# Fixed places for the q/k turns in a hybrid SSM and attention layer, the values' products behind the granule, and V in two tiles

## The chip, the cores and the metric

The kernel runs on one core of a Trainium2 chip. Its time is the device time of one execution in microseconds (us), taken as the median of several runs. A profile is one further execution with the hardware profiler on. PE is the matrix engine (TensorE), with PEld for its weight loads; DVE is VectorE, ACT is ScalarE, POOL is GpSimd, and SP issues most of the transfers.

## The reference

One decoder layer on 512 positions of width 1024, in float32. A state-space branch and an attention branch share one input projection, are gated, summed and projected again.

```python
h = rms_norm(x, norm_w)
u_s, z_s, q, k, v, z_a, r_s, r_a = split(h @ w_in)
y_s = s5_branch(u_s, ...)                         # complex diagonal scan, GELU, GLU
y_s = (y_s * silu(z_s)) @ w_ssm_out
q, k = rope(rms_norm(q, q_norm_w)), rope(rms_norm(k, k_norm_w))   # per head of 64
y_a = dilated_attention(q, k, v)                  # 3 groups x 8 heads
y_a = (y_a * silu(z_a)) @ w_attn_out
x = x + (sigmoid(r_s) * y_s + sigmoid(r_a) * y_a) @ w_o
```

In `dilated_attention`, group 0 looks at the last 128 positions, group 1 at every 4th of the last 512 and group 2 at every 16th of the last 2048 (129 keys each, as far as they exist). The three outputs of a head are combined, weighted by their softmax denominators.

## The kernel before

Precision: each float32 operand of the large products is split into a rounded high part and a low remainder (`split`, lines 106 to 112: ACT writes `w_hi`, DVE `w_lo`), and `mm3` (line 122) makes three products, high by high, high by low and low by high. Line 63 is the helper through which every product is recorded, line 67 the one for every transpose on PE.

Weights come in the order of a list, `plan`. `get_w` (line 180) hands out the next piece and starts the load and the split of pieces up to two further on. The split pieces have three buffers.

The attention part is the loop `for hp in range(NP)` at line 1094, over four pairs of heads. What pair `hp` needs in one turn of the loop:

- `scores(hp)` (line 921): products of q and k (`sps`), then for each block of 128 positions a masked minimum on DVE (line 929) and an exponential on ACT (line 931) into the tile `Pt`. POOL moves the sums between partitions (lines 961 and 978), a short chain on DVE joins the denominators of the groups, and DVE scales `Pt` (line 985). `kind` 0 is group 0, `kind` 1 is the two dilated groups.
- `qk_first` (line 884): q and k of the groups 0 and 1 for the next pair, by `wide_granule` (line 817). A granule has four accumulators `pss[r]` (`pj`, one PSUM bank each, all four of the pool `ps_p`) and runs over four pieces of weights `kq`. One (`kq`, `r`) is called a block here: six products of 512 columns. ACT copies the results into `raws[0]` and `raws[1]` (line 891) and squares them (line 879), DVE sums the squares (line 882), and `qk_norm` (line 834) makes the reciprocal root on DVE (lines 115 to 120, 841), scales (line 846) and rotates on POOL (lines 852 to 857). Only after line 857 is a raw tile ready.
- `qk_second(hp + 1, mid)` (line 896): a second granule with q and k of group 2 and v of the groups 1 and 2. Between its pieces it calls `mid(kq)`, which traces `qk_turn(0, ...)`, `qk_turn(1, ...)` and `values`. Behind the granule, for each `r`, it copies the raw tile (line 903), squares, and copies v into the tile `V` (line 905), then norms.
- `qk_turn` (line 859): turns one raw tile for q (`a` = 0) and k (`a` = 1), four transposes on PE into one PSUM bank each (`qtp`), then a high part by ACT (line 873) and a low part by DVE (line 874).
- `values(hp, Pt, V)` (line 988): eight groups of `Pt` transposes (`ptp`), 30 transposes in all, copied to SBUF by ACT (`ptb`, line 1027) and DVE (line 1029) in turn, and 60 products with V into one accumulator `ot`; then `at` (line 1036) takes the gate.
- `v0_unit` (line 585): v of group 0 for the next pair, a projection into one `pj` bank, turned later by its `finish`; then `qk_turn(2, ...)`.

`qtp`, `ptp`, `vtp` and `sps` share the pool `ps_g`, which has three banks at this stage. `at`, the squares (`qsq`) and the evicted v (`vt`) share the tag `t2k` with six buffers. `V` is one tile with one buffer: the next pair's v can be written only when the last product with the old one is done.

What sets the order: the text is traced in program order, but a planner then fixes each engine's order by going through the program with lengths of its own and giving an engine what is ready and stands first. So a place in the text is a preference, not the place on the engine. `queued()` (line 69) adds an order by hand: what its block traces on PE is issued behind the last PE instruction traced before it. Before the change only the turn of group 1 is queued so.

## Time and profile before

| | |
|---|---|
| median of 3 runs | 737.64 us (736.49 to 738.57) |
| span of the profiled execution | 732.6 us |
| its own time beside the span | not given on the page; the median lies 5.1 us above the span |
| PE busy | 699.6 us, 95% |
| mean granted TensorE clock | 0.993 |
| loop over the pairs | about 434 to 667 us of the span |

The span counts from the first to the last instruction of the profiled execution. The engines' busy times overlap, so they don't add up to it. A row of a timeline has the start, the length, the engine, the line in the code, the operation, the output and inputs by their names in the code, the count, and in brackets the idle time before it with what ended it. A row of waits has the total in us, the count and the longest. In a row of stretches the first number is the length; the engines' busy times with their counts, the granted clock (1.00 is full speed), the share of the DMA engines and GB/s follow.

### The profile page before, as it was taken

To read this page: it belongs to the slowest core of one execution; us is meant where nothing else is said; L and a number is where in the kernel's file an instruction comes from. 1 tells how busy PE (TensorE), PEld (TensorE's weight loads), DVE (VectorE), ACT (ScalarE), POOL (GpSimd) and SP (SyncE) were. 2 spreads that over 40 slices of the span, in tenths; PEclk is the share of its full clock that TensorE was granted. 3 is DMA by queue.
4 is the path that set the end of the run, shared out by engine and by line. 5 is a ranking of instruction groups with operands and counts; after the bars stand their busy time and mean duration, and the time that the engine had idled before them with its cause. 6 is when DMAs were issued, how large, how long until landed. Compare 5 with 4: busy or idle time off the path is not lost.

```text
span 732.6 us, 12680 instructions
## 1 busy us (share of the span) xinstructions
PE 699.6 (95%) x4821; PEld 574.2 (78%) x4821; DVE 457.1 (62%) x912; ACT 314.6 (43%) x631; POOL 191.7 (26%) x346
## 2 busy tenths in 40 slices
PE   2799899999999999999999999999989999999997
PEld 2687688778878787888888888788868877878886
DVE  6759673989946546764335659655664666464832
ACT  6434463332326465442144456537153734443420
POOL 3426540230205343550000316021601250230000
PEclk9999999999999999999999999999999999999999
DMA  8433653564547554455333432222412231326441
GB/s 203 106 96 94 171 144 77 137 149 132 120 131 153 122 103 133 139 168 172 99 100 87 130 87 79 66 58 58 115 31 79 65 89 30 115 73 236 139 144 57
DMA packets 137213, 82.14 MB, mean 112 GB/s; under 512 B 32696, under 2 KB 125632, under 8 KB 137024
## 3 DMA queue, kind: packets, MB, share of 16 engines
q1 hardware_dynamic: 135088, 78.96, 37.5%
q0 software_dynamic: 2048, 2.36, 2.6%
q8 instruction: 38, 0.62, 0.4%
q14 instruction: 23, 0.19, 0.1%
q10 hardware_dynamic: 16, 0.00, 0.0%
HBM read 68.46 MB, written 10.49 MB: 108 GB/s over the span
## 4 chain that ended last, share of the span: by engine, by line
PE 87%; DMA 4%; ACT 3%; DVE 3%; SPq 2%; issue 1%; ACTq 0%
PE pj L63 71%; DMA w_raw<-in_w_in_dram 3%; PE sps L63 3%; PE yps L63 3%; PE ot L63 2%; PE ptp L67 2%; PE kps L63 2%; PE xps L63 1%; PE qtp L67 1%; DMA Uj<-ud 1%; ACT w_hi L108 1%; SPq L442 1%; PE wps L67 1%; ACT qkp L873 1%; DVE w_lo L110 1%
## 5 line engine op out<-in xcount | busy, mean ns | idle before, releaser
L108 ACT ACTIVATE w_hi<-w_raw 128x1024 fp32r<-128x1024 f32 x100 | 106.0, 1061 | 236.8 <-PE pj L63 206.6
L110 DVE TENSOR_TENSOR w_lo<-w_raw,w_hi 128x1024 fp32r<-128x1024 f32 x98 | 124.3, 1268 | 107.9 <-ACT w_hi L108 107.2
L63 PE MATMUL pj<-hT_lo,w_hi 128*128 128x512 f32 (+1 forms) x344 | 132.9, 387 | 3.0 <-DVE hT_lo L251 3.0
L63 PE MATMUL pj<-hT_hi,w_hi 128*128 128x512 f32 (+1 forms) x344 | 132.8, 389 | 2.4 <-ACT V L905 1.4
L63 PE MATMUL pj<-hT_hi,w_lo 128*128 128x512 f32 (+1 forms) x344 | 132.4, 386 | 1.6 <-DVE w_lo L110 1.6
L63 PE MATMUL pj<-w_hi,hT_hi 128*128 128x512 f32 (+1 forms) x288 | 106.5, 372 | 0.0
L63 PE MATMUL pj<-w_lo,hT_hi 128*128 128x512 f32 (+1 forms) x288 | 106.5, 370 | 0.0
L63 PE MATMUL pj<-w_hi,hT_lo 128*128 128x512 f32 (+1 forms) x288 | 106.0, 371 | 0.0
L63 PEld LDWEIGHTS pj<-hT_lo,w_hi 128*128 128x128 f32 x344 | 66.0, 192 | 16.2 <-DVE hT_lo L251 3.9
L63 PEld LDWEIGHTS pj<-hT_hi,w_hi 128*128 128x128 f32 x344 | 65.5, 192 | 16.5 <-ACT V L905 2.1
L63 PEld LDWEIGHTS pj<-hT_hi,w_lo 128*128 128x128 f32 x344 | 65.9, 192 | 15.4 <-DVE w_lo L110 2.3
L63 PEld LDWEIGHTS pj<-w_hi,hT_hi 128*128 128x128 f32 x288 | 54.1, 188 | 10.0 <-issue 0.2
L63 PEld LDWEIGHTS pj<-w_hi,hT_lo 128*128 128x128 f32 x288 | 54.0, 188 | 10.0
L63 PEld LDWEIGHTS pj<-w_lo,hT_hi 128*128 128x128 f32 x288 | 54.0, 188 | 9.8
L931 ACT ACTIVATE Pt<-Pt,st 128x256 f32<-128x256 f32 (+1 forms) x64 | 31.0, 492 | 18.7 <-DVE st L929 18.7
L735 POOL TENSOR_TENSOR kt<-kt,dg 16x128 f32<-16x128 f32 x8 | 4.6, 571 | 125.0 <-ACT kt L734 118.4
L852 POOL TENSOR_TENSOR rt<-qraw,tC 128x256 f32<-128x256 f32 x12 | 14.3, 1189 | 87.7 <-DVE qraw L846 87.4
L739 POOL DMA_DIRECT2D dd<-kt x64 | 33.7, 535 | 2.4 <-POOL kt L735 2.4
L874 DVE SCALAR_TENSOR_TENSOR qkp<-qtp,wcol,qkp 128x512 fp32r<-128x512 f32 (+1 forms) x32 | 23.0, 745 | 13.5 <-ACT qkp L873 13.4
L961 POOL COPY sw<-st 32x4 f32<-32x4 f32 x64 | 12.0, 187 | 73.2 <-ACT Pt L931 70.5
L873 ACT ACTIVATE qkp<-qtp,wcol 128x512 fp32r<-128x512 f32 (+1 forms) x32 | 20.8, 685 | 15.7 <-PE qtp L67 10.4
L277 POOL TENSOR_TENSOR ab<-dd,AT 128x512 f32<-128x512 f32 x16 | 23.0, 1446 | 11.6 <-DVE ab L278 11.6
(263 smaller groups left out, 1289.4 us busy)
## 6 DMA issues: line engine op xcount, KB each, us to landing
w_raw<-in_w_in_dram SPq DMA_DIRECT2D x40, 512.0 KB
w_raw<-in_w_in_dram SPq DMA_DIRECT2D x112, 128.0 KB
w_raw<-in_w_glu_dram SPq DMA_DIRECT2D x8, 512.0 KB
w_raw<-in_w_ssm_out_dram SPq DMA_DIRECT2D x8, 512.0 KB
w_raw<-in_w_o_dram SPq DMA_DIRECT2D x8, 512.0 KB
x_all<-in_x_dram SPq DMA_DIRECT2D x4, 512.0 KB
ud<-uT SPq DMA_DIRECT2D x8, 256.0 KB
Uj<-ud SPq DMA_DIRECT2D x8, 256.0 KB
```

The source lines that it names most:

```text
L63: last[0] = nc.tensor.matmul(*a, **k)
L67: last[0] = nc.tensor.transpose(*a, **k)
L108: act.activation(hi, src, AF.Copy, scale=scale)
L110: e.tensor_tensor(lo, src, hi.bitcast(F32), op=ALU.subtract)
L277: eng.tensor_tensor(tv, a2.unsqueeze(2).broadcast_to(sh), ai, op=ALU.mult)
L442: sp.dma_start(D1[64 * h:64 * h + 64, a], bv[a][h])
L739: pool.dma_start(M[Q * t:Q * t + Q, :, 0:P - Q * t], kt[:, :, t:].rearrange("q g k p -> q g (k p)"))
L852: pool.tensor_tensor(t1, rh[:, :, :, 0:16], cv.broadcast_to([P, NB * 2, 2, 16]), op=ALU.mult)
L873: act.activation(hi, ps[sl], AF.Copy, scale=w)
L874: dve.scalar_tensor_tensor(lo, ps[sl], w, hi.bitcast(F32), op0=ALU.mult, op1=ALU.subtract)
L931: act.activation(o, o, AF.Exp, bias=nm, scale=-1.0, accum_out=st[:, kind, 1, h, b:b + 1])
L961: pool.tensor_copy(sw[32 * r:32 * r + 32, :, :, b], st[32 * b:32 * b + 32, 1, :, :, r])
```

## The change

Three things change, all in the attention loop.

1. `wide_granule` calls `mid(kq, r)` ahead of every block instead of ahead of every piece. `qk_turn` can now trace one half (q or k). The four halves of the turns of group 0 and 1 stand ahead of the blocks (2,3), (3,0), (3,1) and (3,2), each queued behind the block before it on PE, and each of these blocks is queued behind its turn.
2. `values` is traced after `qk_second` as a whole and queued behind the granule. Within it the dilated groups (`kind` 1) come first, so the accumulator starts with them and ends with group 0.
3. `V` becomes two tiles with a tag each: `V[0]` for group 0 and `V[1]` for the dilated groups.

```diff
-            act.copy(V[:, 0].rearrange("p b c -> p (b c)"), pt)
+            act.copy(V[0].rearrange("p b c -> p (b c)"), pt)
...
     def new_v():
-        return big.tile([P, NG, NB, P], F32, name="V", tag="s6a")
+        return (big.tile([P, NB, P], F32, name="V0", tag="s6c"), big.tile([P, 2, NB, P], F32, name="V", tag="s6a"))
...
         for kq in range(4):
-            if mid:
-                mid(kq)
             hi, lo = get_w()
             for r in range(NB):
-                for k in range(2):
-                    kk = 2 * kq + k
-                    mm3(pss[r], th[:, kk, r * P:(r + 1) * P], tl[:, kk, r * P:(r + 1) * P], hi[:, k], lo[:, k],
-                        kk == 0, kk == KT - 1)
+                tied = mid(kq, r) if mid else False
+                with queued() if tied else nullcontext():
+                    for k in range(2):
+                        kk = 2 * kq + k
+                        mm3(pss[r], th[:, kk, r * P:(r + 1) * P], tl[:, kk, r * P:(r + 1) * P], hi[:, k], lo[:, k],
+                            kk == 0, kk == KT - 1)
...
-    def qk_turn(g, raw, QT, KA, KB):
-        for a in range(2):
+    def qk_turn(g, raw, QT, KA, KB, parts=(0, 1)):
+        for a in parts:
...
-            act.copy(V[:, 1:3, r], pss[r][:, 256:512].rearrange("p (g c) -> p g c", g=2))
+            act.copy(V[1][:, :, r], pss[r][:, 256:512].rearrange("p (g c) -> p g c", g=2))
...
-                        first = kind == 0 and b == 0
+                        first = kind == 1 and b == 0 and k == 0
                         pe.matmul(o, v, pts[h][:, (2 * i + k) * P:(2 * i + k + 1) * P], start=first,
-                                  stop=kind == 1 and b == NB - 1 and k == 1, skip_group_check=True)
+                                  stop=kind == 0 and b == NB - 1 and k == 1, skip_group_check=True)
         n = 0
-        for kind in range(2):
+        for kind in (1, 0):
...
-            def mid(kq):
-                if kq == 1:
-                    qk_turn(0, raws[0], *QK)
-                if kq == 2:
-                    with queued():
-                        qk_turn(1, raws[1], *QK)
-                if kq == 3:
-                    values(hp, Pt, V)
+            steps = {(2, 3): (0, 0), (3, 0): (0, 1), (3, 1): (1, 0), (3, 2): (1, 1)}
+
+            def mid(kq, r):
+                if (kq, r) not in steps:
+                    return False
+                g, a = steps[kq, r]
+                with queued():
+                    qk_turn(g, raws[g], *QK, parts=(a,))
+                return True
             raw, V_next = qk_second(hp + 1, mid)
+            with queued():
+                values(hp, Pt, V)
             V = V_next
             finv = v0_unit(hp + 1, V)
             qk_turn(2, raw, *QK)
```

More of the change, by code (lines that the diff above doesn't have):

```diff
@@ L1 @@
 import math
-from contextlib import ExitStack
+from contextlib import ExitStack, nullcontext
 import numpy as np
@@ L598, in v_granule @@
         for b in range(2):
-            act.copy(V[:, 1:3, 2 * b:2 * b + 2], pss[b].rearrange("p (r g c) -> p g r c", r=2, g=2))
+            act.copy(V[1][:, :, 2 * b:2 * b + 2], pss[b].rearrange("p (r g c) -> p g r c", r=2, g=2))
     def new_v():
-        return big.tile([P, NG, NB, P], F32, name="V", tag="s6a")
+        return (big.tile([P, NB, P], F32, name="V0", tag="s6c"), big.tile([P, 2, NB, P], F32, name="V", tag="s6a"))
     scn = big.tile([P, 4096], F32, name="scn", tag="s3")
@@ L866, in qk_turn @@
             if a == 0 or g == 0:
-                parts = [(slice(0, P), QT[0][:, g], QT[1][:, g]) if a == 0 else (slice(0, P), KA[0], KA[1])]
+                ends = [(slice(0, P), QT[0][:, g], QT[1][:, g]) if a == 0 else (slice(0, P), KA[0], KA[1])]
             else:
-                parts = [(slice(64 * h, 64 * h + 64), KB[0][64 * h:64 * h + 64, g - 1, h],
+                ends = [(slice(64 * h, 64 * h + 64), KB[0][64 * h:64 * h + 64, g - 1, h],
                           KB[1][64 * h:64 * h + 64, g - 1, h]) for h in range(2)]
-            for sl, hi, lo in parts:
+            for sl, hi, lo in ends:
                 w = wcol[sl, g, a:a + 1]
@@ L1001, in pv @@
                         if kind == 0:
-                            v = V[:, 0, b - 1 + k, po]
+                            v = V[0][:, b - 1 + k, po]
                             o = ov[po, b]
                         else:
-                            v = V[:, 1 + k, b, po]
+                            v = V[1][:, k, b, po]
                             o = ot[po, b * P:(b + 1) * P]
-                        first = kind == 0 and b == 0
+                        first = kind == 1 and b == 0 and k == 0
                         pe.matmul(o, v, pts[h][:, (2 * i + k) * P:(2 * i + k + 1) * P], start=first,
-                                  stop=kind == 1 and b == NB - 1 and k == 1, skip_group_check=True)
+                                  stop=kind == 0 and b == NB - 1 and k == 1, skip_group_check=True)
         n = 0
-        for kind in range(2):
+        for kind in (1, 0):
             for bb in range(2):
```

## The prediction

> **What bounds the kernel now.** I read the page's busy times first, then who waits for whom on PE from the end of the first granule of head pair 0 to the last values, then the timelines of PE, ACT, DVE and POOL there.
>
> ```profile
> span 732.6 us, 12680 instructions
> PE 699.6 (95%) x4821; PEld 574.2 (78%) x4821; DVE 457.1 (62%) x912; ACT 314.6 (43%) x631; POOL 191.7 (26%) x346
> ...
> PE qtp L67 <- DVE qkp L874: 3.5, 2, 1.8
> PE pj L63 <- ACT V L905: 1.4, 3, 0.5
> PE ptp L67 <- DVE qkp L874: 1.0, 2, 0.5
> ```
>
> PE is the bound, and the change alters no matrix product, so it can only win PE's pauses in this stretch or add to them. The three waits are all that PE has here: two for the turns (qtp) of pairs 1 and 2, two at the start of the values' transposes (ptp), and three of 0.47 us in which the next projection waits for a copy into V: 5.9 us in all. Head pair 1 (hp 1 in the loop; it makes the q, k, v of pair 2) shows where they sit. PE:
>
> ```profile
> 523.68 0.39 PE L63 MATMUL pj<-w_hi,hT_hi 128*128 128x512 f32 x1
> ...
> 530.22 0.39 PE L63 MATMUL pj<-w_lo,hT_hi 128*128 128x512 f32 x1
> 530.45 0.39 PE L63 MATMUL pj<-w_hi,hT_lo 128*128 128x512 f32 x1
> 530.68 1.47 PE L67 MATMUL qtp<-ident,qraw 128*128 128x128 f32 x12
> 533.91 0.66 PE L67 MATMUL qtp<-ident,qraw 128*128 128x128 f32 x4 [1.76 <-DVE qkp L874]
> 535.60 0.98 PE L67 MATMUL ptp<-ident,Pt 128*128 128x128 f32 x7 [0.48 <-DVE qkp L874]
> ...
> 544.28 0.50 PE L63 MATMUL pj<-hT_hi,w_hi 128*128 128x512 f32 x1 [0.47 <-ACT V L905]
> ```
>
> All 96 products of the second granule run first; then all 16 turn transposes in one go. `ps_g` has three banks, so the fourth group of four waits until DVE has emptied one. A block (`kq`, `r`) is 6 products 0.233 us apart (530.22, 530.45), 1.4 us. Five blocks before 530.68 puts block (2,3) at 523.68.
>
> The same stretch as sums, for pair 1 and pair 2, and the values of pair 3, whose transposes have projections between them:
>
> ```profile
> 530.68:544.28 13.60, 10.88 (x108) 8.40 (x106) 7.75 (x11) 7.93 (x17) 0.04 (x1) 1.00 0.16 45
> 601.09:615.58 14.49, 11.77 (x107) 9.24 (x106) 7.76 (x11) 7.92 (x17) 0.04 (x1) 0.88 0.13 38
> 605.70:609.11 3.41, 3.10 (x13) 2.36 (x13) 2.22 (x4) 1.63 (x4) 0.00 (x0) 0.50 0.31 93
> 534.57:543.85 9.28, 8.75 (x90) 1.00 0.19 53
> 659.27:667.20 7.93, 7.93 (x94) 1.00 0.35 97
> ```
>
> The first number is the length, the next PE's busy time, the 0.88 and 0.50 the granted clock. Pair 2 takes 0.89 us longer than pair 1: after its pause the clock was halved for 3.41 us. The values take 9.28 us in pair 1 and, with no pause, 7.93 us in pair 3, so some 0.9 us of pair 1's are small pauses that the busy time covers.
>
> **The change, part by part.**
>
> *Order of turns and blocks.* Nothing is added or removed: 16 transposes per pair, four of which now stand before each of the blocks (2,3), (3,0), (3,1), (3,2). What a split costs shows in pair 0, where the planner had split them by itself:
>
> ```profile
> 455.83 0.60 PE L67 MATMUL qtp<-ident,qraw 128*128 128x128 f32 x4
> 456.19 0.48 PE L63 MATMUL pj<-w_hi,hT_hi 128*128 128x512 f32 x1
> 456.50 0.39 PE L63 MATMUL pj<-w_lo,hT_hi 128*128 128x512 f32 x1
> ...
> 450.54 0.74 POOL L857 TENSOR_TENSOR qraw<-rt,rt 128x256 f32<-128x256 f32 x1
> ...
> L873 ACT ACTIVATE qkp<-qtp,wcol 128x512 fp32r<-128x512 f32 (+1 forms) x32 | 20.8, 685 | 15.7 <-PE qtp L67 10.4
> L874 DVE SCALAR_TENSOR_TENSOR qkp<-qtp,wcol,qkp 128x512 fp32r<-128x512 f32 (+1 forms) x32 | 23.0, 745 | 13.5 <-ACT qkp L873 13.4
> L108 ACT ACTIVATE w_hi<-w_raw 128x1024 fp32r<-128x1024 f32 x100 | 106.0, 1061 | 236.8 <-PE pj L63 206.6
> L110 DVE TENSOR_TENSOR w_lo<-w_raw,w_hi 128x1024 fp32r<-128x1024 f32 x98 | 124.3, 1268 | 107.9 <-ACT w_hi L108 107.2
> ```
>
> Four cost 0.36 us (456.19 less 455.83) and the next product 0.08 us more (0.31 against 0.233): 0.44, four times 1.76 us. In the row of twelve above (1.47 us) a group of four comes to 0.49 at most. So nothing. With 1.84 us from group to group, three banks hold each for 5.5 us; ACT and DVE take 0.69 + 0.75 us and may stand behind a weight split of 1.06 + 1.27 us: 3.8. The bank wait of 1.76 us goes, in two pairs: -3.5 us. The wait of 0.48 us at the values is the same queue: -1.0 us.
>
> *What is late next.* The turn now holds PE at (2,3) until raw 0 is normalised, with no other work that PE may take. In pair 0 it is there at 451.3, long before. In pair 1:
>
> ```profile
> 512.63 0.17 DVE L841 TENSOR_SCALAR qv<-ssq 128x32 f32<-128x32 f32 x1
> 514.21 2.05 DVE L985 TENSOR_SCALAR Pt<-Pt,sd 128x128 f32<-128x128 f32 x8
> 519.57 0.62 DVE L985 TENSOR_SCALAR Pt<-Pt,sfb 128x256 f32<-128x256 f32 x2
> 522.63 2.36 DVE L846 TENSOR_TENSOR qraw<-qraw,qrstd 128x1024 f32<-128x1024 f32 x2
> ...
> 526.51 1.73 POOL L857 TENSOR_TENSOR qraw<-rt,rt 128x256 f32<-128x256 f32 x1
> 529.98 0.74 POOL L857 TENSOR_TENSOR qraw<-rt,rt 128x256 f32<-128x256 f32 x1
> ```
>
> Raw 0 is ready at 528.24, raw 1 at 530.72; (2,3) is due at 523.68. As it stands, PE would wait 4.56 us here. The norm took 15.6 us (512.63 to 528.24) because the scaling of `Pt` (L985) stands between its steps. Undisturbed it is shorter. The third norm of the same pair:
>
> ```profile
> 546.10 0.17 DVE L841 TENSOR_SCALAR qv<-ssq 128x16 f32<-128x16 f32 x1
> 549.72 1.23 DVE L846 TENSOR_TENSOR qraw<-qraw,qrstd 128x1024 f32<-128x1024 f32 x1
> 553.76 0.74 POOL L857 TENSOR_TENSOR qraw<-rt,rt 128x256 f32<-128x256 f32 x1
> 557.67 1.04 PE L67 MATMUL qtp<-ident,qraw 128*128 128x128 f32 x8
> ```
>
> 8.4 us. So the wait lies between 4.56 us and none (512.63 + 8.4 = 521.0, 2.6 us early), and the question is whether the scores' softmax still collides with the norm.
>
> *Values traced after the granule, and their `at` with them.* This decides it. ACT in pair 1:
>
> ```profile
> 532.98 1.19 ACT L903 COPY qraw<-pj 128x256 f32<-128x256 f32 x4
> 541.56 0.58 ACT L1027 COPY ptb<-ptp 128x512 f32<-128x512 f32 x1 [1.97 <-PE ptp L67]
> 542.04 0.39 ACT L879 ACTIVATE qsq<-pj 128x256 f32<-128x256 f32 x1
> 543.85 0.37 ACT L905 COPY V<-pj 128x256 f32<-128x256 f32 x1 [1.42 <-PE ot L63]
> ```
>
> The raw copies are done at 534.2, but the first square waits until the last copy of the values, though ACT idles in between, and the other three stand behind the copies into V, which wait for the last product of the values. I read this as: the planner gives out the buffers of one tag (`t2k`) in program order, and `at` of the values came first. In the new text the squares come before `at`, and no longer behind the values. The third norm then starts some 2 us after the granule instead of 2.3 us after the values: 7 to 9 us earlier against the projection that follows. Its turn (557.67, 13.8 us after the values, though its input was there after 10.7) and the scores behind it move forward too; I take 5 us at the least, since the planner's own lengths are unknown. Then the scaling ends by 515.2 instead of 520.2, before L846 can come (512.63 + 3.6 = 516.2), and raw 0 is ready before 523.7. I take no wait, 0 of 0 to 9.1 us (two pairs): the last scaling row is the obstacle, and it moves.
>
> *Dilated groups first, V as two tiles.* V's part for them (V[1]) is free halfway through the values, so the copies into V run beside the other half, the `pj` bank comes free, and the projection starts without the 0.47 us: -1.4 us in three pairs. The products are the same 60 and 30. Behind this now stands ACT: four V copies (4 x 0.37 = 1.5 us) fall into the second half, where `ptb` copies also go; ACT is busy 7.93 of 13.60 us, so it holds.
>
> *The clock.* Pair 2 has only transposes and pauses from 601.1 until its first product after them, 6.6 us, and the clock fell within these:
>
> ```profile
> 607.70 0.69 PE L63 MATMUL ot<-ptb,V 128*64 128x128 f32 x2
> ```
>
> That stretch goes: -0.9 us, bounds 0 and -1.8 (in other runs none or both pairs). [...]
>
> *What comes back at the values' start.* At the granule's end ACT now has a weight split, a raw copy and a square ahead of the first `ptb` copy, in place of the turn's scalings. From the rows: 1.06 + 0.30 + 0.39 = 1.8 us, then 0.58 us: the first bank comes free about 2.4 us after the first transposes began, and the fourth group asks for it after 1.3 (three times 0.44). That is 1.1 us; pair 1 has 0.9 us of hidden pauses there already. Bounds for all pairs: -2.7 us (values like pair 3's) to +5.4 (ACT's 1.8 us in full, three times); I take +0.7.
>
> Sum: -3.5 - 1.0 - 1.4 - 0.9 + 0.7 = -6.1 us, on a profiled span of 732.6 us. The median of the runs, 737.64, lies 5.1 us above that span (the page gives the span alone); I take that as constant: 731.5, and 0.5 us more for a wait at raw 0 that may remain: **732.0 us**.
>
> **The rivals.**
>
> *PE waits for raw 0 (slower).* Place: transposes before (2,3) in pairs 1 and 2. If the scores do not move forward, each costs 4.56 us: -6.1 + 9.1 = +3.0, and the half clock stays, 0.9 to 1.8 us: 741 to 742.5. It decides from 3 us of wait per pair. For it: the rows 523.68 against 528.24. Against: the squares at 542.04, which nothing holds any more. [...]
>
> *The gain moves to the values (no change).* If norm and squares, now first in line on DVE and ACT, hold up the values' `ptb` copies by 2 us in each of three pairs, 6 us come back: 737.
>
> *Better.* With V free early, projections fill the values as in pair 3: 9.28 becomes 7.93, and with the turns' 1.76 pair 1 costs 9.7 of 13.60, pair 2 9.7 of 14.49; -3.9 - 4.8 - 0.5 = -9.2: 728.4.
>
> **How the numbers follow.** Forecast (729.8 to 735) 0.48, better 0.14, no change 0.18, slower 0.20. A change of 0.3%, 2.2 us, is about what a measurement of this kernel can tell from none. Faster: 0.48 + 0.14 and a few of the no-change cases that keep more than 2.2 us: 0.64; same 0.16; slower 0.20. The range takes in the better case and the edge of the slower: 728.4 to 740.0. The forecast's own range is 729.8 to 735.
>
> **What will show it.** Right: qtp in groups of four between pj before (3,3), no wait of theirs for L874; squares right behind the raw copies (L903) and before the values' end; the turn of group 2 fewer than 13 us after the values; L985 before L846; no wait of pj for L905; no 0.50 clock after 600. Wrong: a wait of qtp for POOL's L857 of 1 to 5 us in pairs 1 and 2; ptp or ot waiting for ptb; L985 still between the steps of the first norm.

## The result, and the profile after

| | before | after |
|---|---|---|
| median | 736.49 us (734.70 to 738.88, 9 runs) | 741.00 us (738.80 to 742.85, 9 runs) |
| span of the profiled execution | 732.6 us | 738.7 us |
| mean granted clock over the timed runs | not on record for these nine; 0.990 to 0.992 in six later sets | 0.990 |

The changed kernel is slower: the ratio is 1.0057, with an interval of 1.0039 to 1.0075. The forecast was 732.0 us, with a range of 728.4 to 740.0.

First the busy times on the page of the changed kernel:

```profile
span 738.7 us, 12666 instructions
...
PE 705.6 (96%) x4821; PEld 576.1 (78%) x4821; DVE 455.6 (62%) x912; ACT 315.9 (43%) x631; POOL 185.8 (25%) x346
```

PE is still the bound. The times of the other engines barely move. PE's waits between 420 and 680 us (total, count, longest):

```profile
PE ptp L67 <- DVE ptb L1029: 2.8, 3, 0.9
PE ptp L67 <- ACT ptb L1027: 2.5, 3, 0.8
PE qtp L67 <- POOL qraw L857: 1.4, 2, 0.7
```

All three rows of before (5.9 us) are gone, as forecast. In their place stand two pauses at the values' start in each of three pairs, 5.3 us, and a rest of the wait for raw 0, 1.4 us. That is 0.8 us more waiting, and doesn't explain 6.1 us of span.

So I went through PE's starts from the turn ahead of the loop to the last product of the values, and took from each step, start to start, the usual step of that kind of instruction (its tenth percentile). What is left over, by the kind of work around it, adds up to the whole difference:

| us above the usual step | before | after | difference |
|---|---|---|---|
| score products and the changes to and from them | 8.2 | 11.3 | +3.2 |
| values: transposes, products, changes | 22.0 | 27.3 | +5.3 |
| turns of q and k | 3.8 | 0.6 | -3.2 |
| projections among themselves | 3.2 | 4.8 | +1.6 |
| length of the stretch | 239.4 | 246.3 | +6.9 |

(The stretch begins 0.8 us earlier in the changed kernel, which leaves the 6.1 of the span.)

The place that costs most, pair 1 of the changed kernel, in rows of PE, ACT and DVE:

```profile
534.92 0.60 PE L67 MATMUL qtp<-ident,qraw 128*128 128x128 f32 x4
535.66 0.67 ACT L873 ACTIVATE qkp<-qtp,wcol 64x512 fp32r<-64x512 f32 x1
536.37 0.74 DVE L874 SCALAR_TENSOR_TENSOR qkp<-qtp,wcol,qkp 64x512 fp32r<-64x512 f32 x1
536.75 1.03 PE L67 MATMUL ptp<-ident,Pt 128*128 128x128 f32 x8
537.22 0.67 ACT L879 ACTIVATE qsq<-pj 128x256 f32<-128x256 f32 x2
537.76 1.07 ACT L108 ACTIVATE w_hi<-w_raw 128x1024 fp32r<-128x1024 f32 x1
537.98 0.68 DVE L1029 COPY ptb<-ptp 128x512 f32<-128x512 f32 x1
538.72 0.66 PE L67 MATMUL ptp<-ident,Pt 128*128 128x128 f32 x4 [0.93 <-DVE ptb L1029]
538.85 0.68 ACT L873 ACTIVATE qkp<-qtp,wcol 64x512 fp32r<-64x512 f32 x1
539.55 1.07 ACT L1027 COPY ptb<-ptp 128x512 f32<-128x512 f32 x2
540.20 0.66 PE L67 MATMUL ptp<-ident,Pt 128*128 128x128 f32 x4 [0.82 <-ACT ptb L1027]
540.24 0.76 DVE L874 SCALAR_TENSOR_TENSOR qkp<-qtp,wcol,qkp 64x512 fp32r<-64x512 f32 x1
```

The last half-turn (534.92) is the k half of group 1, which has two scaling pairs (a high part by ACT and a low part by DVE), one for each head. Only one block stands between it and the values. The planner issued block (3,3), which is tied to nothing, earlier: 12 products stand between the second and the third half-turn. The second of them, L873 at 538.85 and L874 at 540.24, stands behind squares and a weight split. So the half-turn holds its bank from 534.92 to 541.00. The values have two banks instead of three, and their first copy by ACT comes at 539.55, 2.8 us after their first transposes. From start to start the two pauses are 1.09 and 0.99 us, 2.08 a pair and 6.2 in all, where before had about 1.5 in all (0.65 in each of pairs 1 and 2, 0.2 in pair 0).

Raw 0 in the same pair. The scaling of `Pt` is done early now, but ahead of the norm, not behind it:

```profile
513.99 1.66 DVE L985 TENSOR_SCALAR Pt<-Pt,sfb 128x256 f32<-128x256 f32 x6
515.56 0.69 DVE L882 TENSOR_REDUCE ssq<-qsq 128x8 f32<-128x512 f32 x1
516.15 1.22 DVE L110 TENSOR_TENSOR w_lo<-w_raw,w_hi 128x1024 fp32r<-128x1024 f32 x1
517.29 0.18 DVE L841 TENSOR_SCALAR qv<-ssq 128x32 f32<-128x32 f32 x1
...
520.29 1.23 DVE L110 TENSOR_TENSOR w_lo<-w_raw,w_hi 128x1024 fp32r<-128x1024 f32 x1 [1.26 <-ACT w_hi L108]
522.33 2.36 DVE L846 TENSOR_TENSOR qraw<-qraw,qrstd 128x1024 f32<-128x1024 f32 x2
527.96 0.66 PE L67 MATMUL qtp<-ident,qraw 128*128 128x128 f32 x4 [0.68 <-POOL qraw L857]
```

The norm begins at 517.29 (512.63 before) and raw 0 is ready at 527.9: 10.6 us instead of 15.6.

The scores did move forward, and that has its price. All score products of the kernel, before and then after (the first number behind the bar is the busy time):

```profile
L63 PE MATMUL sps<-qkp 128*128 128x256 f32 (+2 forms) x192 | 22.0, 287 | 0.0
```

```profile
L63 PE MATMUL sps<-qkp 128*128 128x256 f32 (+2 forms) x192 | 25.8, 287 | 0.0
```

The same 192 products take 3.8 us longer. The products of group 0 use half of the rows, head 0 the one half and head 1 the other. Before, twelve of both heads run alternately and their successor starts 0.90 us later; after, six of one head take as long, 0.89 us:

```profile
508.44 0.97 PE L63 MATMUL sps<-qkp 64*128 64x256 f32 x12
509.34 0.50 PE L63 MATMUL pj<-w_hi,hT_lo 128*128 128x512 f32 x1
```

```profile
500.55 0.96 PE L63 MATMUL sps<-qkp 64*128 64x256 f32 x6
501.44 0.50 PE L63 MATMUL pj<-w_hi,hT_hi 128*128 128x512 f32 x1
```

The row of 0.50 us shows what stands behind the +1.6 of the projections: the first projection behind transposes, behind the values' products or behind these scores steps 0.08 to 0.11 us wider than the next ones. In the stretch projections begin anew 33 times before and 55 times after, and 12 of the 22 more are behind turns. Behind a turn this is no loss: from the last transpose to the first projection PE takes 0.03 us instead of the usual 0.109, so the table books to the turns what it charges to the projections, 1.0 us. A real price of about 0.6 us is left, behind scores and values.

The clock, at last. Here are two stretches of 3.4 us behind the values' pauses of pairs 0 and 2 (the number after the engines is the granted clock):

```profile
468.20:471.60 3.40, 3.40 (x24) 2.30 (x23) 1.96 (x8) 0.48 (x1) 0.00 (x0) 0.55 0.53 154
611.90:615.30 3.40, 3.40 (x23) 2.41 (x22) 1.69 (x8) 0.48 (x1) 0.00 (x0) 0.50 0.54 154
```

The profile of before has one such window in the loop. In the changed kernel the values take 16.19 us in pairs 0 and 2, from the first transpose to the last product, and 14.67 in pair 1, where the clock is whole; before, 9.85 us in pair 2 and 8.96 in pair 1. So about 2.2 us of the profiled +5.3 in the values are clock (two times 1.52, less 0.89). Over the timed runs there is little of it: 0.990 against 0.990 to 0.992.

### The profile page after: what moved, and what is told of

Same layout as the page of the kernel before. It is cut to its first block, busy times and chain, and to the rows that moved or that the text cites. A ratio compares the mean times of both kernels' runs of the same rounds, so it can differ in the third digit from the quotient of the medians.

```text
span 738.7 us, 12666 instructions
## 1 busy us (share of the span) xinstructions
PE 705.6 (96%) x4821; PEld 576.1 (78%) x4821; DVE 455.6 (62%) x912; ACT 315.9 (43%) x631; POOL 185.8 (25%) x346
## 4 chain that ended last, share of the span: by engine, by line
PE 84%; DVE 4%; ACT 3%; DMA 3%; issue 3%; SPq 2%; POOL 1%; POOLq 0%; ACTq 0%
PE pj L63 67%; PE sps L63 3%; PE ot L63 3%; PE yps L63 3%; DMA w_raw<-in_w_in_dram 2%; PE ptp L67 2%; PE kps L63 2%; PE qtp L67 1%; PE xps L63 1%; DVE w_lo L110 1%; ACT w_hi L108 1%; SPq L442 1%; PE wps L67 1%; DMA Uj<-ud 1%; SPq L216 1%
## 5 line engine op out<-in xcount | busy, mean ns | idle before, releaser
L110 DVE TENSOR_TENSOR w_lo<-w_raw,w_hi 128x1024 fp32r<-128x1024 f32 x98 | 126.2, 1288 | 86.1 <-ACT w_hi L108 85.7
L852 POOL TENSOR_TENSOR rt<-qraw,tC 128x256 f32<-128x256 f32 x12 | 12.2, 1016 | 141.5 <-DVE qraw L846 141.2
L874 DVE SCALAR_TENSOR_TENSOR qkp<-qtp,wcol,qkp 128x512 fp32r<-128x512 f32 (+1 forms) x32 | 23.5, 747 | 17.6 <-ACT qkp L873 17.2
L873 ACT ACTIVATE qkp<-qtp,wcol 128x512 fp32r<-128x512 f32 (+1 forms) x32 | 21.3, 684 | 25.1 <-PE qtp L67 19.4
L63 PEld LDWEIGHTS sps<-qkp 128*128 128x128 f32 (+1 forms) x192 | 22.8, 187 | 5.1 <-issue 2.9
```

The lines of the kernel that those rows point to most:

```text
L63: last[0] = nc.tensor.matmul(*a, **k)
L110: e.tensor_tensor(lo, src, hi.bitcast(F32), op=ALU.subtract)
L852: pool.tensor_tensor(t1, rh[:, :, :, 0:16], cv.broadcast_to([P, NB * 2, 2, 16]), op=ALU.mult)
L873: act.activation(hi, ps[sl], AF.Copy, scale=w)
L874: dve.scalar_tensor_tensor(lo, ps[sl], w, hi.bitcast(F32), op0=ALU.mult, op1=ALU.subtract)
```

## The experiments

Each timed run has its span and its mean granted clock. Their product is my estimate of the time that the run would have at full clock; it separates the order of the work from the clock. The kernel before has 726.1 to 726.8 us by it, in every set of runs. The sets ran on different chips, each with the kernel before beside it, so compare kernels by the ratio or by span x clock and not by the medians.

| kernel | median, us | ratio to before, interval | span x clock | clock |
|---|---|---|---|---|
| after | 741.00 | 1.0057, 1.0039 to 1.0075 | 731.5 | 0.990 |
| values first | 742.15 | 1.0091, 1.0063 to 1.0118 | 730.8 | 0.987 |
| values first, own `at` | 739.74 | 1.0065, 1.0037 to 1.0093 | 732.0 | 0.991 |
| turns one block later | 739.91 | 1.0051, 1.0030 to 1.0073 | 732.8 | 0.993 |
| paired scores | 749.13 | 1.0183, 1.0151 to 1.0215 | 736.0 | 0.985 |
| k first in group 1 | 734.02 | 0.9986, 0.9970 to 1.0002 | 727.9 | 0.994 |
| no fixed places | 734.47 | 0.9996, 0.9977 to 1.0015 | 728.3 | 0.994 |
| V split alone | 735.27 | 0.9997, 0.9976 to 1.0018 | 725.2 | 0.990 |
| own `at` alone | 735.74 | 1.0011, 0.9990 to 1.0031 | 727.5 | 0.991 |
| two blocks behind | 732.76 | 0.9980, 0.9958 to 1.0001 | 726.4 | 0.994 |
| no fixed places, k first | 739.16 | 1.0078, 1.0049 to 1.0107 | 730.2 | 0.990 |
| fixed turns alone | 743.50 | 1.0134, 1.0097 to 1.0170 | 731.9 | 0.987 |
| whole turns | 733.18 | 0.9990, 0.9971 to 1.0009 | 726.2 | 0.994 |
| late whole turns | 734.43 | 0.9980, 0.9966 to 0.9995 | 728.1 | 0.994 |
| late whole turns, split on POOL | 738.02 | 1.0022, 1.0005 to 1.0040 | 731.4 | 0.994 |
| long stretch | 739.85 | 1.0074, 1.0046 to 1.0102 | 733.4 | 0.994 |
| control of it | 744.86 | 1.0133, 1.0101 to 1.0165 | 737.0 | 0.993 |
| pauses filled | 745.52 | 1.0144, 1.0121 to 1.0167 | 736.7 | 0.990 |

My theories at first: the last half-turn's own scalings make the pause at the values' start (C); the buffer of `at` decides whether the scores move forward (T2K). The rivals: the pause comes from the squares and the weight split; the values' place in the text decides by due times.

**Values first**, the values traced right behind the granule, ahead of raw copies and squares:

```diff
         pss = wide_granule(hT_hi, hT_lo, mid)
+        if then:
+            with queued():
+                then()
```

> The changed kernel, with the values traced right behind the second granule and ahead of its raw copies, squares and copies into V (still queued behind the granule on PE). Theory A: the 6 us are lost at the values' start, where each of three pairs waits 2.1 us in two pauses for the first copies of the transposed Pt, because squares, square sums and a weight split stand ahead of them; and the squares are early only because the buffer of `at` is asked for after theirs. Then these two pauses shrink to 0.3 to 0.7 us a pair (-4 to -5 us), but the squares wait for the values again, the scores move back, the wait for raw 0 in pairs 1 and 2 grows from 1.1 to 4 to 5 us (+7), and the split scores go together again (-3): about 741, the wait for raw 0 clearly above 3 us. Theory B (the order of the requests for buffers has nothing to do with it): raw 0 as in the changed kernel, pauses smaller, 736 to 737.

**Values first, own `at`**, the same with another buffer for `at`:

```diff
-        at = t2k("at")
+        at = gate_tile() if hp < NP - 1 else t2k("at")
```

> As the run with the values traced ahead of the copies, but `at` of the first three pairs takes a buffer of the gate's tag instead of the one that the squares use. Theory A: squares no longer held, so raw 0 is as early as in the changed kernel (wait at most 1.1 us), while the first copies of the transposed Pt come ahead of squares and norm: pauses 0.3 to 0.7 us a pair: 736 to 737.5. Theory B (requests for buffers do not matter): the same as the other run. Theory C (the pauses come from the turns' own scalings and the weight split): pauses stay at 1.5 to 2.1 us a pair, 740 to 741.

PE's waits with the values first, and then with a buffer of its own for `at`:

```profile
PE qtp L67 <- POOL qraw L857: 6.8, 2, 3.4
PE ptp L67 <- DVE ptb L1032: 2.4, 3, 0.8
PE ptp L67 <- ACT ptb L1030: 1.3, 3, 0.4
```

```profile
PE ptp L67 <- DVE ptb L1032: 2.8, 3, 0.9
PE ptp L67 <- ACT ptb L1030: 2.5, 3, 0.8
PE qtp L67 <- POOL qraw L857: 1.3, 2, 0.7
```

T2K holds: one buffer moves the wait for raw 0 from 6.8 to 1.3 us, with the text's order the same. The scores go with it: 8.2 us above the usual step with the squares held, 11.3 with the own buffer, exactly the pair of numbers of before and after. So the 3.2 us are the price of early scores. The pauses with the own buffer are those of the changed kernel to a tenth: where the squares stand in the text is not their cause. With the squares held until the values are done (the first of the two runs) the pauses are 0.95 and 0.59 us, 1.54 a pair instead of 2.08. So about 0.5 us a pair comes with the squares, and the larger part doesn't.

**Turns one block later:**

```diff
-            steps = {(2, 3): (0, 0), (3, 0): (0, 1), (3, 1): (1, 0), (3, 2): (1, 1)}
+            steps = {(3, 0): (0, 0), (3, 1): (0, 1), (3, 2): (1, 0), (3, 3): (1, 1)}
```

> The changed kernel with the four half turns one block later, ahead of (3,0), (3,1), (3,2) and (3,3). Theory A: the wait for raw 0 in pairs 1 and 2 (1.1 us each) goes, but the last turn's scalings end one block nearer to the values, and the first pause there grows by up to 1 us in each of three pairs: 739 to 742. Theory C (the last turn's scalings make the pauses): the pauses grow by the whole 1.4 us a pair, 743 or more. If the wait for raw 0 were the main loss: 738.5 or less.

PE waited 3.6 us for raw 0, not less but more. In pair 1 its norm takes 11.0 us from L841 to the end of L846 where the changed kernel has 7.4: the last scaling of `Pt` and two weight splits more stand among its steps. What put them there isn't shown. The pause was 1.8 us a pair: it shrank, where theory C had it grow by 1.4. The trace shows that the run didn't test this, for one block stands between the last half-turn (536.35) and the values (538.18), as in the changed kernel.

**Paired scores**, group 0's products chained in the order of the text:

```diff
+                        with queued() if i + n + h else nullcontext():
+                            pe.matmul(pss[h][:, cols], QT[x_][po, 0, cb], KA[y_][po, ks], start=n == 0, stop=n == 2,
```

> The changed kernel, with the products of the scores of group 0 chained, so that those of the two heads (64 rows of the array each) alternate again. In the changed kernel 12 of them run as 6 and 6 of one head, 0.89 us each, against 0.97 us for 12 of both heads in the kernel before. Theory A: that costs 0.9 us in each of pairs 1 to 3, so 738 to 739. Rival: the projections between them take the time anyway, or PE now waits at the first product of the second head: 741.

A miss. The scores' share fell only from 11.3 to 10.8 us, they ended later, and PE waited 6.3 us for raw 0. In the trace the first product of each twelve now stands alone, 0.9 to 4.5 us ahead of the other eleven, and takes 0.25 to 0.31 us there. As I read it, twelve in a row must wait for two banks where six wait for one, so that the sixes cost less than their cure.

**K first in group 1**, the last two half-turns exchanged:

```diff
-            steps = {(2, 3): (0, 0), (3, 0): (0, 1), (3, 1): (1, 0), (3, 2): (1, 1)}
+            steps = {(2, 3): (0, 0), (3, 0): (0, 1), (3, 1): (1, 1), (3, 2): (1, 0)}
```

> The changed kernel with its last two half-turns exchanged: at (3, 1) the k half of group 1, at (3, 2) its q half. The last half-turn ahead of the values is then one of one scaling pair (one ACT scaling, one VectorE subtraction) instead of two. Theory C (the pause at the values' start is the last half-turn's own scalings, which hold one of the three banks and stand ahead of the values' first copies): the pause of 2.08 us in each of three pairs falls to about 1.0, so some 3 us less than the changed kernel: about 738. Rival (the pause comes from the squares and the weight split on ACT): unchanged, 741. Both: the wait for raw 0 stays within 1.3 to 1.6 us in all.

```profile
PE ptp L67 <- DVE ptb L1029: 1.5, 3, 0.6
PE qtp L67 <- POOL qraw L857: 1.4, 2, 0.7
```

C holds for the larger part of the pause. The pauses fall from 6.2 to 2.9 us, start to start, by exchanging two entries; span x clock falls by 3.7. The time falls by more, since the clock rises from 0.990 to 0.994, 3 us of 732. The loop has no halved window left:

```profile
427.00:667.00 240.00, 236.90 (x1371) 190.41 (x1370) 148.02 (x406) 121.05 (x291) 58.51 (x167) 1.00 0.25 73
```

**No fixed places**, turns traced as before, V split and values behind the granule kept:

```diff
-            steps = {(2, 3): (0, 0), (3, 0): (0, 1), (3, 1): (1, 0), (3, 2): (1, 1)}
+            steps = {(1, 0): (0, 0), (2, 0): (1, 0)}
...
-                with queued():
-                    qk_turn(g, raws[g], *QK, parts=(a,))
-                return True
+                with queued() if g else nullcontext():
+                    qk_turn(g, raws[g], *QK)
+                return False
```

> The changed kernel without its fixed places: both turns are traced where the kernel before has them, group 1 queued; V stays two tiles and the values still follow the granule, dilated groups first. Theory (the fixed places cost at the values' start, the placing of the values gives the early scores): no pause of 1 us at the values' start (below 0.5 a pair, so about -4.7 us), the early turns wait for banks again (0 to 3.5 us as in the kernel before), raw 0's wait stays about 1.4 us, scores of one head in sixes as in the changed kernel: 736 to 739. Rival (the values' place alone is what costs, by the split scores and by ACT's crowding): 740 to 742 with pauses of 1 us or more a pair still there.

No wait for raw 0 and none of a turn, but one pause of 1 us a pair was still there (2.5 us listed in all), against the expectation of less than 0.5. The time is that of before, so the slowdown in time needs the fixed places. But the order of the work is still 2.2 us longer by span x clock (728.3 against 726.1), which a higher clock hides. By this measure the changed kernel is 4.7 to 5.4 us above before: its fixed places cost about 3 us, and what is left here, with the early scores, about 2.

**V split alone**, the kernel before with V as two tiles and the dilated groups first:

> The kernel before with only V in two tiles and the dilated groups first; values and turns are traced where the kernel before has them. Theory: the V copy's wait of 1.4 us goes, the squares are still held until the gated tile of the same pool is released, so scores stay where they were in twelves; no wait for raw 0 is new: 735 against 736.2. Rival (dilated groups first lets the planner start values earlier and they meet the turns' banks): bank waits grow by the 1.4 or more, 736 to 738.

The three waits for the copy into V are gone, the turns' waits stay (3.5 and 0.8 us), and scores stay in twelves. Span x clock is 0.8 us under before, somewhat less than the 1.4 expected; in the time this can't be told from nothing. Of the change's parts it is the one that brought no new wait, and so the new place of the values costs about 3 us by span x clock (+2.2 without fixed places, less this -0.8).

**Own `at` alone**, the kernel before with the buffer of the run above:

> The kernel before with only a buffer of its own for the gated tile of the values in pairs 0 to 2, so that the squares need not wait for it. Theory T2K (buffers of that pool are given in the order of the text, and the gated tile held the squares): first squares then stand right behind the raw copies, the turn of group 2 and its scores move forward by several us, scores of group 0 run in sixes as in the changed kernel (+1 to 1.6 us a pair), bank waits as before: 735 to 739. Rival (the values' place in the text holds the norm by its due times and not by the buffer): squares, turn and scores stay where they were, 736.

T2K holds here too. The squares stand right behind the raw copies, in pair 1 at 534.54 us (542.04 before):

```profile
534.54 0.40 ACT L879 ACTIVATE qsq<-pj 128x256 f32<-128x256 f32 x1
```

The turn of group 2 begins 18.7, 12.2 and 18.3 us after the values' first transpose, where before has 22.7, 23.1 and 24.0: it moved forward in every pair. Only one pair ran group 0 in sixes, and the scores' share was 9.5 us, between the two.

**Two blocks behind the last half-turn**, which is q of group 1 right after its k:

```diff
+            steps = {(2, 3): (0, (0,)), (3, 0): (0, (1,)), (3, 1): (1, (1, 0)), (3, 2): (0, ()), (3, 3): (0, ())}
```

> As the run with k first in group 1, and its q half follows the k half at once at (3, 1); the blocks (3, 2) and (3, 3) are chained behind it, so that two blocks of 6 products stand between the last half-turn and the values, not one. If what is left of the pause at the values' start in that run (0.45 us in pair 0, 1.22 in pairs 1 and 2, start to start) is the last scaling pair, it falls below 0.3 a pair, some 2 us in all, and the time to about 732 (734.0 for the run with k first). Rival: what is left is the split of the weights for the next granule (ACT 1.08 us, then VectorE 1.22 us between the values' first copies): pauses stay at 1 us a pair in pairs 1 and 2, and the time at 734. Both: raw 0 is waited for as before (1.4 us listed in all); no new wait of a half-turn for a bank.

```profile
PE ptp L67 <- DVE ptb L1029: 1.8, 3, 0.6
PE qtp L67 <- POOL qraw L857: 1.3, 2, 0.7
```

Between the two: the pause is 0.78 us a pair, start to start, in all three pairs. No row of the last half-turn stands ahead of it any more. What PE waits for is VectorE's first copy, which stands behind the square sum of the granule's last block:

```profile
534.56 0.42 DVE L882 TENSOR_REDUCE ssq<-qsq 128x4 f32<-128x256 f32 x1 [0.88 <-ACT qsq L879]
535.01 0.69 DVE L1029 COPY ptb<-ptp 128x512 f32<-128x512 f32 x1
```

**No fixed places, k first** (the edit is against the run without fixed places):

```diff
-                    qk_turn(g, raws[g], *QK)
+                    qk_turn(g, raws[g], *QK, parts=(1, 0) if g else (0, 1))
```

> As the run without fixed places, with group 1's turn traced k first, so that its last half is of one scaling pair. Theory C: the pause at the values' start (1.09, 0.95 and 0.95 us a pair, start to start, with that run) falls by about 0.7 a pair, 2 us in all: 732.5 against 734.5. Rival: the pause there is the weights' split, as above: same time, 734.5. Raw 0 isn't waited for in either.

A miss: 1.0078 against 0.9996 without k first, where a gain was expected. Left to itself the planner puts no block between the last half-turn and the values. The q half's one pair then came ahead of the values' copies on ACT and behind the weight split on DVE, and the pauses grew to 2.55 us and more in pairs 1 and 2. K first helps only with a block behind it.

**Fixed turns alone**, the kernel before with the fixed half-turns. V is one tile. The values moved as well: they are traced behind the granule, ahead of the raw copies, and not queued:

> The kernel before with the half-turns in fixed places alone: V is one tile, undilated group first, and the values are traced behind the granule ahead of the raw copies, not queued. The squares are then held by the gated tile (as with the values first), so raw 0 is waited for by 3.4 us in each of pairs 1 and 2 and the scores stay late and in twelves; the last half-turn's two scaling pairs give the pause of about 1.5 to 2 us a pair at the values' start; the turns' bank waits of 3.5 us are gone. Sum against before: +6.8 +3 -4.5: 741 to 742. Rival (the pause needs the dilated order): pause below 0.7 a pair, 738 to 739.

```profile
PE qtp L67 <- POOL qraw L857: 6.8, 2, 3.4
PE ptp L67 <- ACT ptb L1029: 2.0, 3, 0.7
PE ptp L67 <- DVE ptb L1031: 2.0, 3, 0.7
PE pj L63 <- ACT V L907: 1.4, 3, 0.5
```

As expected in each term. The sum expected was 5.3 us; span x clock gives 5.4 (731.9 against 726.4). The time rose by more, since the clock fell to 0.987. So this order costs as much without the early scores, by the wait for raw 0. In the changed kernel the values behind the squares take 5.4 us of that wait away again (6.8 to 1.4), and bring the early scores.

**Whole turns**, q and k of group 0 at (2, 3), k and q of group 1 at (3, 1):

> As the run with k first, but each turn whole in one place: group 0 (q, k) at (2, 3), group 1 (k, q) at (3, 1); the planner's order then has the last half-turn 6 products ahead of the values, and group 0's turn 18 products ahead instead of 30. Expected: raw 0's wait falls from 1.7 us (start to start, both pairs) to below 0.3, since its turn starts two blocks later; two fewer changes between products and transposes a pair (0.1 us each); the pause at the values' start unchanged at 0.45 to 1.2: 732 against 734. Rival: raw 0 is itself late by the same two blocks, since its norm hangs on PE's progress (as in the run with the turns one block later): the wait stays or grows, 734 to 736.

No wait for raw 0 is left. Eight smaller waits, 2.5 us in all, stand in the values. Span x clock is 1.7 us lower than with k first (726.2 against 727.9), as expected for the time; the ratio to before, 0.9990, can't be told from that run's 0.9986.

**Late whole turns**, both findings together:

```diff
+            steps = {(3, 0): (0, (0, 1)), (3, 1): (1, (1, 0)), (3, 2): (0, ()), (3, 3): (0, ())}
```

> Both findings in one kernel: as the run with two blocks behind the last half-turn, but group 0's turn stands whole one block later, at (3, 0), so that 24 products lie between its start and the values instead of 30. Theory (the pause at the values' start and the wait for raw 0 are separate terms and add up): pauses stay at the 0.78 us a pair of that run (start to start), the wait for raw 0 (0.84 us in each of pairs 1 and 2) falls to below 0.3, the half-turns wait for no bank by more than 0.3: 731 against 732.8 and about 0.4% under the kernel before. Rival (raw 0 is coupled to PE's progress): the wait stays at 0.8, 732.8.

```profile
PE qtp L67 <- DVE qkp L874: 2.3, 3, 0.8
PE ptp L67 <- DVE ptb L1029: 1.9, 3, 0.6
```

The two terms don't add up: with eight transposes, one block and eight more, the fourth half-turn waits for a bank, 0.8 us in each of three pairs, which is what the wait for raw 0 had cost in two pairs. It is still the one version whose interval lies wholly below the kernel before (0.9966 to 0.9995), by 0.2%. Among so many versions one such interval can be chance. All of the gain is clock: by span x clock it is 1.3 us above the 726.8 that the kernel before had beside it.

**Late whole turns, split on POOL**, the same kernel with the low part of the next weights moved from VectorE:

```diff
+            lo_w[0] = pool
             finv = v0_unit(hp + 1, V)
+            lo_w[0] = dve
```

> As the run just before it, and the low part of the weights that VectorE splits between the values' first two copies (L110, 1.22 us) goes to POOL (2.35 us there). Theory S (the pause that is left is the square sum of the granule's last block, which stands ahead of the first copy on VectorE): pause unchanged at about 0.78 a pair, time within 1 us of the run just before. Rival W (it is this split): pause below 0.2 a pair, 2 us less. Against both: the split on POOL could hold the rotation of raw 2 back, which would show as a wait of group 2's turn.

The pause is unchanged at 0.78 us, so the weights' split isn't its cause. That it is the square sum, I read in the trace; it wasn't tried. The time rose by 3.6 us, which neither theory had: see the last section.

**Long stretch** and **its control**, the run with two blocks and 28 transposes a pair made a second or third time, ahead of the values' first product or between the later ones:

```diff
+                            for _ in range(1 + ((2 if n else 1) * (n < 4)) * (hp < NP - 1)):
+                                pe.transpose(ps[:, (2 * i + k) * P:(2 * i + k + 1) * P],
```

> The run with two blocks behind the last half-turn, and in pairs 0 to 2 some transposes of the values' first four groups are made again into the same place: 28 more a pair, all ahead of the values' first product. Their results are the same; only PE's stretch without a product there grows, from 2.7 us to about 4.8. Theory H (the clock halves only behind a stretch of about 3.9 us or more without a product; so far behind 15 of 22 such stretches and behind none of 31 shorter ones): halved windows appear in the loop behind most of the three stretches, and the mean granted clock over the timed runs falls from 0.9937 to about 0.989. Time: 28 times 0.109 us less the pause of 0.78 that they cover, 2.3 us a pair, 7 in all, and 3 to 5 us by the clock: 743 to 745. Rival (the pauses do it, or chance): the clock stays at 0.993 to 0.994, 740.

> The control: the same kernel with 28 more transposes a pair in the values' last four groups, between products, so that no stretch without a product is longer than about 2.8 us. Theory H: no halved window in the loop, mean granted clock 0.993 to 0.994; time 28 times 0.109 us in three pairs more, 9.2: 742. Rival (more transposes as such lower the clock): 0.989 as in the other run, 745.

Theory H fell: both runs have a clock of 0.993 to 0.994, and the one meant to be slowed by it is the faster. (The control's time is 3 us above what was expected, by span x clock 1.4; what made that isn't shown.) In the long stretch PE makes nothing but transposes for 4.9 us in each of three pairs, and the clock stays whole. Two of them:

```profile
535.60:540.50 4.90, 4.90 (x45) 4.73 (x43) 3.36 (x11) 2.79 (x5) 0.00 (x0) 1.00 0.05 13
606.90:611.80 4.90, 4.90 (x45) 4.72 (x43) 3.54 (x12) 2.78 (x5) 0.00 (x0) 1.00 0.05 12
```

**Pauses filled**, the changed kernel with repeated transposes where PE waits for banks:

> The changed kernel, with 16 transposes a pair made again into the place that they have filled already (pairs 0 to 2): 8 of the values' first group behind the second, 8 of the third group behind itself, where PE waits for banks. Nothing of the result changes; PE is given something to do in the two pauses of 1.09 and 0.99 us. Theory I (formed after the last two runs: what halves the clock is PE's idle time close together, 2.1 us or more within 3.4 us; in the profiles so far 15 of 22 places with that much are followed by a halved window, and none of those with 1.97 us or less): the idle time at the values' start falls below 1 us, no halved window is left in the loop, the mean granted clock of the timed runs rises from 0.990 to 0.993 or 0.994. Time: 2.5 us or so less by the clock with 16 transposes more, and the planner's order of the scores moves as well: 737 to 739. Theory H (stretch without a product) has fallen. Rival (no such rule): clock 0.990, 741.

```profile
PE qtp L67 <- POOL qraw L857: 6.4, 2, 3.2
```

The pauses at the values' start are gone, and no halved window follows there in any of three pairs. But the planner moved the scores back by it, PE waited 3.2 us for raw 0 in pairs 1 and 2, and a halved window follows the one of pair 2. So the mean clock stayed at 0.990 and the time was a miss. The other pause of 3.35 us, in pair 1, is followed by none, though it is as long; what spared it isn't shown. The run doesn't show what the clock alone would give.

## Why the prediction was wrong

*Waits that go* (-3.5, -1.0, -1.4 us): right. None of the three rows is left, and the run with V split alone shows the last for itself.

*What comes back at the values' start* (+0.7 us): the step that failed most. The pauses there came to 6.2 us where before had about 1.5, the 1.0 above among them: the term should have been +5.7, just beyond its upper bound of +5.4. The prediction put a weight split, a raw copy and a square ahead of ACT's first copy "in place of the turn's scalings". They came in addition to them: the last half-turn stands one block before the values, and one of its two scaling pairs fell behind all that, so that it held one of the three banks. The exchange of q and k took 3.3 us of it away. About 0.5 us a pair comes with the squares. That a square sum makes the 0.78 us a pair which two blocks leave was read in the trace and not tried.

*Scores move forward at no cost* (no term): the second step that failed. They moved, for the reason given (the buffer of `at`), which the pair of runs shows. But PE then ran group 0 in sixes: +3.2 us.

*Splitting the turns costs "nothing"*: right. The first projection behind a half-turn steps 0.08 us wider, and the step into it is 0.08 us shorter. What the prediction left out are the other new beginnings of projections, behind scores and values: about +0.6 us.

*Raw 0* (none, +0.5 kept): 1.4 us listed, 0.84 each from start to start, 1.7 in all. The scaling left the middle of the norm but went ahead of it, and a weight split stayed inside.

*The clock* (-0.9 us): no gain over the timed runs. The mechanism wasn't borne out either. The prediction put the halving down to 6.6 us with only transposes and pauses; no run shows that such a stretch as a whole halves the clock, and 4.9 us of transposes alone ran at 1.00. Pair 2 lost its old pauses and got new ones of 2.08 us, and the clock behind these was 0.50 again (611.88 to 615.30 us).

*The base*: the prediction put the median 5.1 us above the span as a constant. In 153 of the 159 runs of the kernels in the table a run's own time is 1.7 to 1.9 us above its own span (in six with repeated transposes 2.0 to 2.8). The rest was the draw of the profiled run.

Of the rivals, the slower one named 741 to 742.5 us, the time that was measured, but by 9.1 us of waiting for raw 0, of which 1.4 came: that was luck. The rival "the gain moves to the values" has the mechanism and its size, 2 us in each of three pairs; it stopped at 737 because the price of the early scores was in no step. In the prediction's own terms the sum at full clock is about -5.9 (waits) + 5.7 (values' start) + 3.2 (scores) + 1.7 (raw 0) + 0.6 (new beginnings) = +5.3 us. The table of the first section, less 2.2 us of clock, gives +4.7 us, and span x clock, 731.5 less 726.1 to 726.8, +4.7 to +5.4.

## What to carry to other kernels

Before work is tied closely in front of a stage that shares its buffers, follow the last tied piece to the instruction that frees its buffer, on each engine's queue, and put the piece with the fewest such instructions last, with other work tied behind it: without a block behind it the same exchange made the kernel slower. Exchanging two entries of a table was worth 0.7% here by the ratios, 5.2 us, of which 3 came by the clock, nearly as much as all the waits that the change had removed (5.9 us). When work is moved forward to end a wait, ask what it will be interleaved with where it lands: the same 192 products took 3.8 us longer there.

## What the runs showed of the hardware

What stood ahead of a halved clock was counted in the 19 profiles. I summed PE's pauses (over 0.35 us above the usual step) within any 3.41 us of the loop. With 2.08 us or more, a window of halved clock (0.50) followed at 16 of 24 places; with 0.65 to 1.97 us, at none of 59. At the changed kernel's 2.08 us the longest single pause is 1.09; a halved window followed there in pairs 0 and 2, and none in pair 1, where the clock was 1.00 from 536.7 to 544.0 us. What spared the eight places isn't shown.

In each of the 19 profiles all changes of the granted clock lie whole multiples of 3.413 us apart; in the loop of the changed kernel they are at 468.52, 471.93, 611.88 and 615.30 us. In the long stretch 4.9 us of transposes alone ran at 1.00 (535.60 and 606.90 us). The sum was found in these profiles after the fact, and only one run was made to try it: the counts don't show what makes the clock fall.

Twelve score products of two heads, on different halves of PE's rows and issued alternately, took 0.90 us in the kernel before (508.44 to 509.34 us); six of one head alone took 0.89 in the changed kernel (500.55 to 501.44 us).

With the weights' split on POOL, a step of the norm on VectorE that takes 0.17 us elsewhere lasts until POOL is done, in each of three pairs (2.25 to 2.32 us). Pair 1, where the two end at 542.68 and 542.65 us:

```profile
540.43 2.25 DVE L115 TENSOR_SCALAR qa<-qv 128x16 int32<-128x16 int32 x1
```

```profile
540.30 2.35 POOL L110 TENSOR_TENSOR w_lo<-w_raw,w_hi 128x1024 fp32r<-128x1024 f32 x1 [8.51 <-ACT w_hi L108]
```

VectorE's first copy for the values ends at 540.31 and its next one begins at 543.02, 2.71 us later; in the run with two blocks, where VectorE splits the weights between the two, it is 1.20 us (535.70 to 536.90). PE waits for the copy three times (1.7 us listed). POOL had been idle for 8.51 us ahead of the split, but while the work moved to it ran, VectorE's step took 2.25 us instead of 0.17.
